# A planned order for the expert layer: routing in two parts, one-hots on VectorE, two sums for the gathered rows

## Chip, cores and metric

One Trainium2 chip, one core. The metric is the device time of one execution in microseconds (us), shown as the median of several runs; the lower the better.

## What is computed

Two transformer blocks on one sequence of 256 tokens of width 2048. The first block has two layers (sparse attention beside retention), the second a mixer of two attentions and then PEER, a layer that picks single-neuron experts. The change lies in PEER alone. Cut to what matters:

```python
def peer_sublayer(h, w_query, sub_keys, u, v):       # 256 tokens, 8 heads, 16384 experts
    q = (hb @ w_query).reshape(PEER_BLOCK, 8, 2, 128)
    s = jnp.einsum('thpc,hpnc->thpn', q, sub_keys)    # two halves of 128 keys each
    top_s, top_i = lax.top_k(s, 16)
    cand_s = top_s[:, :, 0, :, None] + top_s[:, :, 1, None, :]
    best_s, best_j = lax.top_k(cand_s.reshape(..., 256), 16)
    idx = take_along_axis(128 * first_half + second_half, best_j)
    g = softmax(best_s)
    a = gelu(einsum('thkd,td->thk', u[idx], hb))
    return einsum('thk,thkd->td', g * a, v[idx])
```

## The kernel before

The work up to the queries (both attention blocks, `first_layer`, `second_mixer`) is ordered by the framework's scheduler, and so is PEER. PEER goes through these steps, in tiles of 128 tokens by `t` in 0 and 1:

- **Queries and routing** (`peer_query`, `peer_route`). Four chunks of the query weight, each split into a high and a low part for exact products (`raw`, `hi`, `lo`, L204 and L205). For each of 16 pairs of head and token tile `peer_route` takes two top-16 of 128 keys (`top16`), adds them to 256 sums, takes their top-16, marks the places (`eq`, a product on GpSimd), reduces to key numbers (`keyno`) and row numbers (`idx`), and makes the softmax weights `gw`. `digit_rows` splits the key numbers into digits for the distance products below.
- **Scores.** The first `GU` = 1024 columns of the table `u` are fetched row by row for the picked experts: `peer_gather_u`, 256 indirect DMAs from GpSimd's queue of 128 rows each (L1307), whose product with `hn` is summed on VectorE (L1315, "dot") or multiplied on GpSimd (L1312) and summed on ScalarE (L1313), by a fixed turn. The last 1024 columns go dense through TensorE: `peer_scores` loads 128 pieces `uraw`, turns each (L259), splits it (`uhi` L1337 on ScalarE, `ulo` L1338 on VectorE) and multiplies (L1340 to L1342) into `S`. The text calls one piece an expert (it holds 128 of them).
- **Picks and weights.** `peer_pick` draws the scores of the picked experts out of `S` by one-hot products (`ohf`, L1359; selection L1363), `peer_coef` makes the coefficients `cf`, and `peer_weights` builds two one-hots per token from distance products on TensorE (L1389, L1395), multiplies them (L1400) and moves the result back over `S` (L1401). 32 groups of four tokens for each `t`.
- **Output.** The table `v` in the same two ways: `peer_gather_v` fetches `GV` = 704 columns by 256 indirect DMAs (L1415) and adds them, weighted, to one sum `vacc`, on VectorE (L1424) or by a scaling on ScalarE (L1421) and an add on GpSimd (L1422), by a fixed turn; `peer_out` loads 128 pieces `vraw` of the other 1344 columns, splits them and `S` (`vhi`, `vlo` L1441, `wh`, `wl` L1445) and multiplies (L1449).

Indirect rows land in rings of buffers that are taken in turn (`gathered_rows`): three, later six. SP's queue issues all plain loads in order. `ahead` mixes gathers into the dense steps at fixed rates, and the scheduler may lift them ahead:

```python
def ahead(self, gather, n=1):
    with self.tc.high_priority(offset=AHEAD):
        for _ in range(n):
            next(gather, None)
```

## Time and profile before

| | before |
|---|---|
| median of 3 runs (lowest, highest) | 3316.0 us (3314.67, 3328.48) |
| the profiled execution's own time | 3326.01 us |
| its span, first to last instruction | 3324.3 us |
| mean granted TensorE clock | 0.945 |
| busy: TensorE, VectorE, ScalarE, GpSimd | 90%, 71%, 48%, 36% |
| moved by DMA | 749.43 MB, 225 GB/s on average |

The profile is of one execution. A busy share is an average over stages with different limits, so it is read by stretch. Where instructions of one engine overlap, its busy time counts the union. In single rows the first number is the start in us from the span's start, the second the duration, then engine, source line, operation and tiles.

### The profile page before, as it was taken

To read this page: it belongs to the slowest core of one execution; us is meant where nothing else is said; L and a number is where in the kernel's file an instruction comes from. 1 tells how busy PE (TensorE), PEld (TensorE's weight loads), DVE (VectorE), ACT (ScalarE), POOL (GpSimd) and SP (SyncE) were. 2 spreads that over 40 slices of the span, in tenths; PEclk is the share of its full clock that TensorE was granted. 3 is DMA by queue.
4 is the path that set the end of the run, shared out by engine and by line. 5 is a ranking of instruction groups with operands and counts; after the bars stand their busy time and mean duration, and the time that the engine had idled before them with its cause. 6 is when DMAs were issued, how large, how long until landed. Compare 5 with 4: busy or idle time off the path is not lost.

```text
span 3324.3 us, 46436 instructions
## 1 busy us (share of the span) xinstructions
PE 2992.6 (90%) x16644; PEld 2519.5 (76%) x16644; DVE 2357.7 (71%) x4263; ACT 1583.7 (48%) x2533; POOL 1205.5 (36%) x861
## 2 busy tenths in 40 slices
PE   3698999799999999999999578889888999999998
PEld 1476667577788779998779567888787778788887
DVE  7879886967766664565558998777554565888886
ACT  5555545545444544454544233433333466555553
POOL 3324432412000000000002645776554346877772
PEclk9699998899999999999999799999998996999999
DMA  8777876767655555544466668999884234999997
GB/s 299 236 248 248 282 252 199 250 188 222 174 165 159 167 163 150 150 139 134 145 226 194 209 222 269 335 341 334 268 275 163 73 114 140 324 330 325 322 335 250
DMA packets 294612, 749.43 MB, mean 225 GB/s; under 512 B 33518, under 2 KB 40612, under 8 KB 293996
## 3 DMA queue, kind: packets, MB, share of 16 engines
q1 hardware_dynamic: 236432, 517.74, 49.0%
q0 software_dynamic: 57344, 226.53, 19.7%
q8 instruction: 131, 2.15, 0.3%
q10 hardware_dynamic: 604, 2.19, 0.2%
q14 instruction: 101, 0.83, 0.1%
HBM read 739.55 MB, written 6.82 MB: 225 GB/s over the span
## 4 chain that ended last, share of the span: by engine, by line
PE 56%; DMA 13%; DVE 13%; POOL 5%; issue 5%; ACT 3%; POOLq 0%; another core or an unknown queue 0%; DVEq 0%; ACTq 0%; SPq 0%
PE b_mm L1449 10%; PE b_mm L231 7%; PE b_mm L230 7%; PE b_mm L232 7%; DMA mraw<-in_w_mod 6%; DMA gathered<-in_peer_u,idx 5%; PE b_at L1359 4%; PE b_at L1449 3%; DVE gathered L1315 3%; PE b_tr L1400 3%; DVE lo L205 2%; PE b_mm L252 2%; PE b_mm L251 2%; PE b_mm L250 2%; POOL gathered L1307 2%
## 5 line engine op out<-in xcount | busy, mean ns | idle before, releaser
L205 DVE TENSOR_TENSOR lo<-raw,hi 128x1024 fp32r<-128x1024 f32 (+2 forms) x488 | 615.0, 1262 | 360.1 <-ACT hi L204 358.1
L204 ACT CAST hi<-raw 128x1024 fp32r<-128x1024 f32 (+2 forms) x488 | 498.8, 1025 | 486.0 <-PE b_mm L232 275.4
L231 PE MATMUL b_mm<-lo,hh 128*128 128x512 f32 (+1 forms) x1536 | 620.3, 404 | 29.6 <-DVE lo L205 29.0
L232 PE MATMUL b_mm<-hi,hl 128*128 128x512 f32 (+1 forms) x1536 | 605.0, 399 | 0.0
L230 PE MATMUL b_mm<-hi,hh 128*128 128x512 f32 (+1 forms) x1536 | 581.6, 402 | 9.0 <-ACT hi L204 6.7
L1342 PE MATMUL b_mm<-hd,ulo 128*128 128x256 f32 x1024 | 315.3, 308 | 80.2 <-DVE ulo L1338 78.9
L1415 POOL DMA_INDIRECT gathered<-in_peer_v,idx x256 | 333.2, 1302 | 144.6 <-DVE vacc L1424 92.3
L231 PEld LDWEIGHTS b_mm<-lo,hh 128*128 128x128 f32 x1536 | 295.5, 192 | 109.8 <-DVE lo L205 50.0
L1307 POOL DMA_INDIRECT gathered<-in_peer_u,idx x256 | 286.5, 1119 | 252.1 <-DVE gathered L1315 140.2
L230 PEld LDWEIGHTS b_mm<-hi,hh 128*128 128x128 f32 x1536 | 293.6, 192 | 84.2 <-ACT hi L204 11.2
L232 PEld LDWEIGHTS b_mm<-hi,hl 128*128 128x128 f32 x1536 | 294.0, 192 | 62.3 <-issue 0.8
L1340 PE MATMUL b_mm<-hd,uhi 128*128 128x256 f32 x1024 | 317.8, 310 | 21.7 <-ACT uhi L1337 20.9
L398 POOL TENSOR_TENSOR macc<-macc,mraw 128x512 f32<-128x512 f32 x112 | 182.2, 1627 | 422.9 <-ACT mraw L396 382.9
L1315 DVE SCALAR_TENSOR_TENSOR gathered<-gathered,hn 128x1024 f32<-128x1024 f32 x196 | 264.1, 1354 | 83.3 <-DMA gathered<-in_peer_u,idx 83.2
L1341 PE MATMUL b_mm<-hd,uhi 128*128 128x256 f32 x1024 | 299.9, 293 | 0.0
L1342 PEld LDWEIGHTS b_mm<-hd,ulo 128*128 128x128 f32 x1024 | 207.0, 202 | 101.0 <-DVE ulo L1338 98.9
L1337 ACT CAST uhi<-b_tr 128x512 fp32r<-128x512 f32 x256 | 148.6, 587 | 260.5 <-PE b_tr L259 224.0
L1338 DVE TENSOR_TENSOR ulo<-b_tr,uhi 128x512 fp32r<-128x512 f32 x256 | 174.3, 687 | 105.1 <-ACT uhi L1337 93.9
L1441 DVE TENSOR_TENSOR vlo<-vraw,vhi 128x1344 fp32r<-128x1344 f32 x128 | 206.8, 1616 | 34.5 <-ACT vhi L1440 31.8
L1340 PEld LDWEIGHTS b_mm<-hd,uhi 128*128 128x128 f32 x1024 | 206.7, 202 | 29.4 <-ACT uhi L1337 27.2
L1341 PEld LDWEIGHTS b_mm<-hd,uhi 128*128 128x128 f32 x1024 | 207.0, 202 | 0.0
L1424 DVE SCALAR_TENSOR_TENSOR vacc<-gathered,cf,vacc 128x704 f32<-128x704 f32 x186 | 177.2, 953 | 19.7 <-POOL vacc L1422 10.4
(608 smaller groups left out, 6248.4 us busy)
## 6 DMA issues: line engine op xcount, KB each, us to landing
raw<-in_w_in SPq DMA_DIRECT2D x336, 512.0 KB
mraw<-in_w_mod SPq DMA_DIRECT2D x192, 512.0 KB
vraw<-in_peer_v SPq DMA_DIRECT2D x128, 672.0 KB
uraw<-in_peer_u SPq DMA_DIRECT2D x128, 512.0 KB
raw<-in_w_out SPq DMA_DIRECT2D x96, 512.0 KB
raw<-in_peer_w_query SPq DMA_DIRECT2D x32, 512.0 KB
raw<-in_w_in SPq DMA_DIRECT2D x16, 256.0 KB
gathered<-in_peer_u,idx POOLq DMA_INDIRECT x256
```

The lines of the kernel that those rows point to most:

```text
L204: nc.scalar.copy(hi[:, :, :n], raw[:, :, :n])
L205: nc.vector.tensor_tensor(lo[:, :, :n], raw[:, :, :n], hi.bitcast(F32)[:, :, :n], ALU.subtract)
L230: nc.tensor.matmul(o, ah[:, kk, s], hi[:, k, :n], start=kk == 0, stop=False)
L231: nc.tensor.matmul(o, ah[:, kk, s], lo[:, k, :n], start=False, stop=False)
L232: nc.tensor.matmul(o, al[:, kk, s], hi[:, k, :n], start=False, stop=kk == KT - 1)
L1307: nc.gpsimd.indirect_dma_start(out=g, out_offset=None, in_=rows, in_offset=bass.IndirectOffsetOnAxis(ap=self.idx[h, t][:, k:k + 1], axis=0))
L1315: nc.vector.scalar_tensor_tensor(g, g, 1.0, self.hn[:, t, :], op0=ALU.mult, op1=ALU.mult, accum_out=o)
L1340: nc.tensor.matmul(o, hi[:, k, :], hh[:, k0 + k, :], start=k0 + k == 0, stop=False)
L1341: nc.tensor.matmul(o, hi[:, k, :], hl[:, k0 + k, :], start=False, stop=False)
L1342: nc.tensor.matmul(o, lo[:, k, :], hh[:, k0 + k, :], start=False, stop=k0 + k == UD - 1)
L1415: nc.gpsimd.indirect_dma_start(out=g, out_offset=None, in_=rows, in_offset=bass.IndirectOffsetOnAxis(ap=self.idx[h, t][:, k:k + 1], axis=0))
L1449: nc.tensor.matmul(acc[t, q][:, :w], a[:, t * P:(t + 1) * P], b[:, c - GV:c - GV + w], start=e == 0 and n == 0, stop=e == P - 1 and n == 2)
```

## The change

From the queries on, the order of every engine's instructions is fixed in the kernel. A new class `Plan` takes each step as an operation with an engine (or a choice of two), a cost, a key of priority, what it follows and which ring of buffers it takes and frees. `Plan.run` keeps one clock per engine and one for DMA, always emits the step that can start first (the smallest key within 0.05 us), and the framework keeps that order (`manual_schedule`).

With it:

- Routing is in two parts (`plan_route`): the two top-16 of a pair go ahead with early keys, the sums and the rest follow with later ones, nine pairs of results deep. Marks are one `eq` of two halves in bf16. The softmax weights are divided once per `t`.
- Products with gathered `u` rows and sums of gathered `v` rows have no fixed turn: the plan chooses between VectorE on the one side and GpSimd with ScalarE on the other. GpSimd's sums of `v` go to a second accumulator, merged at the end. Gather buffers are taken in any order.
- Weights: the two one-hots of a token are made on VectorE by comparing with a row of numbers; their distance products on TensorE are gone, and with them half of the digit rows.
- `GV` goes from 704 to 768, so the dense part of `v` from 1344 to 1280 columns. Five pieces of `u` are loaded ahead into buffers of their own (`PRE`), and the transposes use a second pair of banks from the 17th piece on.

In numbers, from the built order: gather products on VectorE 196 before, 159 now, on GpSimd 60 and 97; `v` adds on VectorE 186 and 100, on ScalarE and GpSimd 70 and 156 (of these 154 adds on GpSimd); query subtractions on GpSimd none and 11 of 32; distance products 512 of 128x128 and none. In the output stage the built order has 93 adds on VectorE and 107 scalings on ScalarE.

```diff
+class Plan:
+    LAT = 0.15
...
+    def run(self):
+        while self.left:
+            best = None
+            for e, ops in self.ready.items():
...
+                first = min(c[0] for c in can) + 0.05
+                c = min((c for c in can if c[0] <= first), key=lambda c: c[1])
+                if best is None or c[0] < best[0]:
+                    best = c
...
+            end = self.clock[e] = t + cost
+            fn(o)
+            self.signal(o.issued, end, e)
+            if kb:
+                self.transfers = max(self.transfers, t) + kb / 340.0
+                end = max(self.transfers + 2.0, end + 3.5)
...
-GV = 704
+GV = 768
...
+        u = plan.op("DVE", 1.75, lambda o: best_half(o, 0), a0, after=[y], takes=[tv])
+        v = plan.op("DVE", 1.75, lambda o: best_half(o, 1), a0, after=[u], frees=[(sc, y)])
+        w = plan.op("DVE", 0.85, sums, b0, after=[v], takes=[cand, two], frees=[(tv, u)])
+        z = plan.op("DVE", 2.4, best_sums, b0, after=[w], frees=[(cand, w)])
+        b = plan.op("DVE", 1.3, places, b0, after=[z], takes=[eq])
+        m = plan.op("POOL", 1.8, marked, b0 - 20, after=[b])
...
-                    if k % (3 if self.gathered < 56 else UOFF if self.gathered < 240 else 2) == 1:
-                        nc.gpsimd.tensor_tensor(g, g, self.hn[:, t, :], ALU.mult)
-                        nc.scalar.activation(g, g, AF.Identity, accum_out=o)
-                    else:
-                        nc.vector.scalar_tensor_tensor(g, g, 1.0, self.hn[:, t, :], op0=ALU.mult,
-                                                       op1=ALU.mult, accum_out=o)
+                plan.choice([("DVE", 1.42, dot, (), 0), ("POOL", 2.5, product, (poolq,), 0)], key, after=[o])
...
-            r1, r, c = self.distance(t, n)
-            p1 = self.bank("mm", 4)
-            for i in range(4):
-                nc.tensor.matmul(p1[:, i * P:(i + 1) * P], r1[:, i * P:(i + 1) * P], c, start=True, stop=True)
+            def second(o, n=n, s=s):
+                s["b"] = self.vp.tile([P, 4, P], F32, name="ohb", tag="ohb", bufs=3)
+                nc.vector.tensor_tensor(s["b"], self.iota[:, None, :].to_broadcast([P, 4, P]),
+                                        self.byexp[t][:, 1, n:n + 4, None].to_broadcast([P, 4, P]), ALU.is_equal)
+            def first(o, n=n, s=s):
+                s["a"] = a = self.vp.tile([P, 4, P], F32, name="oha", tag="oha", bufs=4)
+                for i in range(4):
+                    nc.vector.tensor_scalar(a[:, i, :], self.iota, self.byexp[t][:, 0, n + i:n + i + 1],
+                                            self.byexp[t][:, 2, n + i:n + i + 1], op0=ALU.is_equal, op1=ALU.mult)
...
-                    if k % VOFF == 1 and not (t == 1 and h >= 6):
-                        nc.scalar.activation(g, g, AF.Identity, scale=c)
-                        nc.gpsimd.tensor_tensor(a, a, g, ALU.add)
-                    else:
-                        nc.vector.scalar_tensor_tensor(a, g, c, a, op0=ALU.mult, op1=ALU.add)
+                            plan.op("POOL", 2.05, lambda o: nc.gpsimd.tensor_tensor(a, a, s["g"], ALU.add), key - 12,
+                                    after=[o], frees=[(gv, s["op"]), (poolq, o)], signals=[self.added])
...
+                    plan.choice([("DVE", 1.06, add, (), 0), ("ACT", 0.98, scale, (poolq,), 0)], key,
+                                after=[o, self.cf_done[t][1]])
```

Three places of the built order. First SP's queue of loads, from the last weights of the mixer to the score table (`raw` are weights of the mixer and of the queries, `uraw` and `upre` pieces of the score table). Before:

```order
L199 DMA raw<-in_w_out 128x2x512 x10
L1327 DMA uraw<-in_peer_u 128x1024 x3
L199 DMA raw<-in_w_out 128x2x512 x22
L199 DMA raw<-in_peer_w_query 128x2x512 x5
...
L1175 DMA x_kept<-x 128x4096
...
L199 DMA raw<-in_peer_w_query 128x2x512 x27
L1327 DMA uraw<-in_peer_u 128x1024 x24
```

Now:

```order
L355 DMA raw<-in_w_out 128x2x512 x32
L1457 DMA raw<-in_peer_w_query 128x2x512 x3
...
L1332 DMA x_kept<-x 128x4096
...
L1711 DMA upre_14666<-in_peer_u 128x1024
L1711 DMA uraw<-in_peer_u 128x1024 x3
L1457 DMA raw<-in_peer_w_query 128x2x512 x29
L1711 DMA uraw<-in_peer_u 128x1024 x33
```

Five pieces `upre` and three `uraw` now stand behind the first three query weights.

Second, VectorE where routing and scores share it (`ulo` is the score subtraction, `gathered` the product with a gathered row, `cand`, `best`, `bj`, `eq`, `keyno`, `idx` belong to routing). Before:

```order
L1315 SCALAR_TENSOR_TENSOR gathered,act_14636<-gathered,hn 128x1024
L1500 CAST bf__16425<-bj 128x32
L1221 TENSOR_SCALAR dig<-dig 128x128
L1338 TENSOR_TENSOR ulo<-b_tr,uhi 128x512
L1504 TENSOR_TENSOR eq<-bf__16425,iota_14622 128x256 x2
L1222 TENSOR_SCALAR dig<-dig 128x128
L1338 TENSOR_TENSOR ulo<-b_tr,uhi 128x512
```

Now:

```order
L1575 TENSOR_REDUCE keyno_14631<-eq 128x2x16
L1578 SCALAR_TENSOR_TENSOR idx<-keyno_14631 128x16
L1579 TENSOR_SCALAR idx<-idx 128x16
L1731 TENSOR_TENSOR ulo<-b_tr,uhi 128x512
L2018 MAX best<-cand 128x8
L2019 MAX_INDEX bj<-best,cand 128x8
L2021 MATCH_REPLACE cand<-best,cand 128x256
L2018 MAX best<-cand 128x8
L2019 MAX_INDEX bj<-best,cand 128x8
L1731 TENSOR_TENSOR ulo<-b_tr,uhi 128x512
```

Before, 49 `ulo` and 50 products stand ahead of the last `idx`; now 72 `ulo` and 11 products. GpSimd has 43 gathers and 30 products ahead of its last mark, and 215 gathers of `u` ahead of the first of `v`.

Third, GpSimd in the output stage. Before:

```order
L1415 DMA gathered<-in_peer_v,idx 128x704 x3
L1422 TENSOR_TENSOR vacc<-vacc,gathered 128x704
L1415 DMA gathered<-in_peer_v,idx 128x704 x4
L1422 TENSOR_TENSOR vacc<-vacc,gathered 128x704
L1415 DMA gathered<-in_peer_v,idx 128x704 x3
```

Now:

```order
L1921 TENSOR_TENSOR vacc_22893<-vacc_22893,gathered 128x768
L1902 DMA gathered<-in_peer_v,idx 128x768 x2
L1921 TENSOR_TENSOR vacc_22893<-vacc_22893,gathered 128x768
L1902 DMA gathered<-in_peer_v,idx 128x768
L1921 TENSOR_TENSOR vacc_22893<-vacc_22893,gathered 128x768
```

An add stood behind every third or fourth gather; now behind every one or two, and it has a sum of its own. Of the 64 weight groups on TensorE 18 stand between picks and 46 behind the last pick.

## Rows read from the trace of the kernel before

**Rows 1.** Busy time of each engine by stretch (us from the span's start):

```profile
core 0: us, PE busy (x) PEld busy (x) DVE busy (x) ACT busy (x) POOL busy (x), PEclk, DMA share, GB/s
1740.00:2037.00 297.00, 223.97 (x1646) 211.86 (x1646) 265.79 (x818) 105.03 (x203) 143.56 (x116) 0.90 0.65 212
2037.00:2541.00 504.00, 435.89 (x3323) 415.18 (x3324) 331.35 (x525) 188.82 (x340) 310.84 (x230) 0.94 0.86 303
2541.00:2626.00 85.00, 82.95 (x351) 60.73 (x350) 43.13 (x292) 30.07 (x54) 15.68 (x11) 0.94 0.15 46
2626.00:2743.00 117.00, 115.77 (x735) 91.28 (x736) 74.03 (x276) 70.24 (x101) 63.02 (x54) 0.96 0.43 124
2743.00:2828.00 85.00, 80.74 (x518) 69.17 (x516) 42.50 (x65) 56.01 (x78) 52.54 (x42) 0.64 0.49 142
2828.00:3314.00 486.00, 481.59 (x2304) 405.09 (x2304) 405.04 (x395) 257.08 (x302) 345.50 (x226) 0.99 0.91 318
```

**Rows 2.** Timeline of TensorE, scores: transpositions of one half piece each:

```profile
2305.57 0.60 PE L259 MATMUL b_tr<-ident,uraw 128*128 128x128 f32 x4
...
2309.32 0.60 PE L259 MATMUL b_tr<-ident,uraw 128*128 128x128 f32 x4
```

**Rows 3.** The chain that ended last, 2330 to 2400 us: shares, one piece:

```profile
by line: DMA gathered<-in_peer_u,idx 55.6%; issue 11.7%; DVE gathered L1315 11.4%; POOL gathered L1312 7.0%; POOL gathered L1307 5.4%; DVE ulo L1338 2.7%; PE b_mm L1342 2.7%; PE b_mm L1340 2.0%; PE b_mm L1341 1.9%; PE b_tr L259 1.9%; ACT uh
...
2338.75 8.72 DMA gathered<-in_peer_u,idx
```

**Rows 4.** Groups by line, 2037 to 2541 us (busy, mean ns | idle before):

```profile
L1307 POOL DMA_INDIRECT gathered<-in_peer_u,idx x186 | 209.7, 1128 | 170.9 <-DVE gathered L1315 117.9 <-issue 32.0 <-ACT gathered L1313 9.1
L1315 DVE SCALAR_TENSOR_TENSOR gathered<-gathered,hn 128x1024 f32<-128x1024 f32 x146 | 198.7, 1370 | 65.5 <-DMA gathered<-in_peer_u,idx 65.5
L1338 DVE TENSOR_TENSOR ulo<-b_tr,uhi 128x512 fp32r<-128x512 f32 x208 | 141.5, 688 | 105.1 <-ACT uhi L1337 93.9 <-issue 9.0 <-ACT S L1344 1.6
```

**Rows 5.** The page's 40 slices; tile raw: ns min/median/max, first and last start:

```profile
GB/s 299 236 248 248 282 252 199 250 188 222 174 165 159 167 163 150 150 139 134 145 226 194 209 222 269 335 341 334 268 275 163 73 114 140 324 330 325 322 335 250
...
L205 DVE TENSOR_TENSOR lo<-raw,hi x488: 135/1225/3006, 35.6 to 1855.6; 128x1024 fp32r<-128x1024 f32 x156, 128x672 fp32r<-128x672 f32 x5, 128x16 fp32r<-128x16 f32 x2
```

**Rows 6.** Picks (group, 2541 to 2626 us), weight products (timeline), a tensor_scalar (group):

```profile
L1359 PE MATMUL b_at<-S,ohf 128*128 128x128 f32 x288 | 71.9, 406 | 0.5 <-ACT ohf L1356 0.5
...
2692.95 1.16 PE L1400 MATMUL b_tr<-ohb,oha 128*128 128x128 f32 x8
...
2748.32 2.08 PE L1400 MATMUL b_tr<-ohb,oha 128*128 128x128 f32 x8 [0.47 <-DVE ohb L1391]
...
L1224 DVE TENSOR_SCALAR digf<-digf 128x128 f32<-128x128 f32 x4 | 0.9, 216 | 0.0
```

**Rows 7.** Timelines of VectorE and GpSimd, each at two places:

```profile
2089.66 3.24 DVE L1315 SCALAR_TENSOR_TENSOR gathered<-gathered,hn 128x1024 f32<-128x1024 f32 x1
2093.44 1.21 DVE L1315 SCALAR_TENSOR_TENSOR gathered<-gathered,hn 128x1024 f32<-128x1024 f32 x1
...
2898.76 1.56 DVE L1441 TENSOR_TENSOR vlo<-vraw,vhi 128x1344 fp32r<-128x1344 f32 x1 [0.45 <-ACT vhi L1440]
2901.19 0.98 DVE L1445 TENSOR_TENSOR wl<-S,wh 128x256 fp32r<-128x256 f32 x1 [0.88 <-PE b_at L1449]
...
2089.40 2.41 POOL L1312 TENSOR_TENSOR gathered<-gathered,hn 128x1024 f32<-128x1024 f32 x1
...
2899.59 2.30 POOL L1422 TENSOR_TENSOR vacc<-vacc,gathered 128x704 f32<-128x704 f32 x1 [0.40 <-ACT gathered L1421]
```

**Rows 8.** Groups by line, 2828 to 3314 us, output stage:

```profile
L1441 DVE TENSOR_TENSOR vlo<-vraw,vhi 128x1344 fp32r<-128x1344 f32 x128 | 206.8, 1616 | 34.5 <-ACT vhi L1440 31.8 <-issue 2.7
...
L1424 DVE SCALAR_TENSOR_TENSOR vacc<-gathered,cf,vacc 128x704 f32<-128x704 f32 x136 | 129.8, 955 | 6.8 <-DMA gathered<-in_peer_v,idx 6.6
L1422 POOL TENSOR_TENSOR vacc<-vacc,gathered 128x704 f32<-128x704 f32 x47 | 94.2, 2003 | 32.1 <-ACT gathered L1421 30.5 <-DVE vacc L1424 0.7 <-issue 0.5
...
L1445 DVE TENSOR_TENSOR wl<-S,wh 128x256 fp32r<-128x256 f32 x128 | 87.0, 680 | 40.8 <-PE b_at L1449 31.8 <-ACT wh L1444 8.7
```

More of the change, by code (lines that the diff above doesn't have):

```diff
@@ L1 @@
-import itertools
 import math
@@ L44 @@
 GU = D - UD * P
-GV = 704
+GV = 768
 GMAX = max(GU, GV)
+FOUR = [P, 2, TOPK, TOPK]
+PRE = 5
+URAW = 3
 UBUFS = 3
-AHEAD = 100
-VOFF = 3
-UOFF = 6
-FIRST = 16
+VRAW = 4
 _INS = (
@@ new lines, in open_scores, with open_more, leave_ud @@
+    def open_scores(self, o):
+        self.st.close()
+        self.st = ExitStack()
+        self.S = self.pool(self.st, "Sp").tile([P, P, T], F32, name="S")
+    def open_more(self, o):
+        self.qs.close()
+        self.rg = self.pool(self.st, "rg")
+        self.gu.add([(self.rg, "g%d" % i) for i in range(3)], self.plan.now)
+    def leave_ud(self, o):
+        more = [s for s in self.gu.slots if s[1][0] is self.rg]
+        self.gu.slots = [s for s in self.gu.slots if s[1][0] is self.ud]
+        self.gu.retire(self.plan, self.left_ud)
+        self.gu.slots += more
@@ L1285, in ahead @@
-    def ahead(self, gather, n=1):
-        with self.tc.high_priority(offset=AHEAD):
-            for _ in range(n):
-                next(gather, None)
-    def gathered_rows(self):
-        turn = itertools.chain.from_iterable([r] * r[1] for r in self.rings)
-        pool, n = next(itertools.islice(turn, self.turn % sum(n for _, n in self.rings), None))
-        self.turn += 1
-        return pool.tile([P, GMAX], F32, name="gathered", tag="g", bufs=n)
-    def peer_gather_u(self):
-        nc = self.nc
-        self.gathered = self.turn = 0
-        rows = self.I["peer_u_2"][0].rearrange("n (c w) -> (n c) w", w=UNIT)
+        return self.rows[p, 512 * h:512 * h + 512], self.digits[p, 4 * t + q, :]
@@ L1303, in peer_gather_u, with plan_gather_v @@
+    def plan_gather_v(self, units, chosen):
+        nc, plan, gv = self.nc, self.plan, self.gv
+        rows = self.I["peer_v_2"][0].rearrange("n (c w) -> (n c) w", w=UNIT)
+        n, last = 0, [chosen]
+        poolq = self.ring("poolv", 2)
         for t in range(2):
@@ new lines, in plan_gather_v, with plan_out, start @@
+                    s["op"] = o = plan.op("POOL", 1.08, gather, key - 25, after=last, takes=[gv], kb=GV / 2)
+                    last = [o.issued]
+                    plan.choice([("DVE", 1.06, add, (), 0), ("ACT", 0.98, scale, (poolq,), 0)], key,
+                                after=[o, self.cf_done[t][1]])
+                    n += 1
+    def plan_out(self, opened):
+        nc, plan, ring = self.nc, self.plan, self.ring
+        cols = [(c, min(512, D - c)) for c in range(GV, D, 512)]
+        acc = {}
+        wide = D - GV
+        def start(o):
@@ L1453, in peer_out @@
-            for _ in gather:
-                pass
-            for t in range(2):
-                for q, (c, w) in enumerate(cols):
-                    y = vp.tile([P, D - GV], F32, name="y", tag="vraw", bufs=4)[:, :w]
-                    nc.sync.dma_start(y, self.x_kept[:, t, c:c + w])
-                    nc.vector.tensor_tensor(y, y, acc[t, q][:, :w], ALU.add)
-                    nc.sync.dma_start(self.out[0, t * P:(t + 1) * P, c:c + w], y)
-                nc.sync.dma_start(self.out[0, t * P:(t + 1) * P, :GV], self.vacc[:, t, :])
+        first = plan.op("ctl", 0, start, 0, after=[opened], takes=[ring("mm", 4)] * 4 + [ring("at", 2)] * 2)
```

934 lines of the change are left out of this document (647 added, 287 removed).

## The prediction, made before the changed kernel was run

> **What bounds the kernel now.** I read the stretches first, then in each of them the groups and single rows of the work that paces it. The change starts at the queries (1740 us), and the built order of all five engines is unchanged ahead of them, so 1740 us stay. Behind them come three stages [rows 1]: queries, routing and scores to 2541 (801 us), picks and weights to 2828 (287 us), the output stage to 3314 (486 us), and 10 us of stores.
>
> In the first, VectorE is busy for 266 of the 297 us to 2037 and TensorE for only 224: with routing and score work in one queue, only some 25 of 128 experts are scored by then (in the built order 49 score subtractions stand ahead of the last routing instruction). Between 2037 and 2541 neither is full: TensorE 436 of 504, DMA at 303 GB/s. Where TensorE is fed, one expert passes in 3.75 us, from one transposition to the second next [rows 2], but 104 experts took 504 us, 4.85 each. The chain of waits names the cause: more than half of a stretch there is landing time of gathered rows [rows 3]. The 186 gathers of this stretch [rows 4] are 2.71 us apart; six buffers make that a loop of 6 x 2.71 = 16 us from one use of a buffer to its next.
>
> In the output stage TensorE is busy for 482 of 486 us: it sets the pace, with DMA close behind at 318 GB/s.
>
> **The change, part by part.** *Queries and routing to 2000 us.* In the new order the first halves of the routing stand ahead of the scores and the second halves between them; 72 score subtractions, 36 experts, now stand ahead of the last routing instruction, and 11 gather products of VectorE instead of 50. The queries themselves keep their 118 us to 1858 (the last weight split starts at 1855.6 [rows 5]). On SP's queue eight pieces of the score table, 4.2 MB, now stand behind the first three query weights and ahead of the other 29 (now three of them stand further ahead), 14 us at 303 GB/s; I take nothing for them, since TensorE works on the three pieces and VectorE, not TensorE, ends this stretch, and 14 us as the upper end. What VectorE has left of the routing at 1858: of its 266 us take 32 query subtractions at 1.23 = 39, 50 products at 1.37 = 68 and 49 score subtractions at 0.68 = 33 [rows 4]; 126 remain for routing and normalisation, and some six tenths of the routing instructions now stand behind the first score, about 75 us. With 72 x 0.68 = 49 and 11 x 1.37 = 15 that is 139 us, against TensorE's 36 x 3.75 = 135. So 36 experts are done near 2000, where now there are 25 at 2037.
>
> *Scores to 2415 us.* 92 experts remain. GpSimd has issued 43 of the 256 gathers by then and 215 before the first gather of the next table: 172 in this stretch. By TensorE alone 92 x 3.75 = 345 us. By DMA: 92 + 172 pieces of 0.524 MB = 138 MB, 457 us at the 303 GB/s of now and 406 at the 341 that the best slice of the profile's page shows [rows 5]. By the loop of buffers, at 2.71 us, 466. A buffer is now taken as soon as the plan has it free, not in turn, and VectorE does 131 products instead of 196 before the picks, so I put the loop nearer to the DMA's end: 415 us, ends 345 and 466. First stage 675 us (now 801): **minus 126**.
>
> *Picks and weights.* The picks keep their instructions: the first stretch had 36 of them (288 half matmuls of eight to a pick [rows 6]) in 85 us, 2.36 each, so 64 cost 151. For the weights the 512 distance matmuls go, and the products stay: eight half matmuls take 1.16 us at full clock and 2.08 at half clock [rows 6]. The granted clock was 0.96 where picks and weights alternated and 0.64 where weights stood alone [rows 1]. In the new order 18 groups of four tokens stand between picks and 46 behind the last: 18 x 1.16 + 46 x 2.08 = 117. VectorE makes the one-hots: four tensor_scalar of 128x128, nearest row 0.216 us [rows 6], and one 128x512, nearest row 0.68 [rows 4], 1.55 us a group. It is hidden under 2.08; were the clock full, it would pace the last 46 groups, 71 us in place of 96. Sum 268, I take 265; ends 240 and the 287 of now: **minus 22**.
>
> *Output stage.* The table's direct part shrinks from 1344 to 1280 columns and the gathered part grows from 704 to 768. TensorE's 482 us become 482 x 1280/1344 = 459. But in the built order only 56 of the 256 gathered rows are added before the stage, so 200 are left in it: 128 x 0.655 + 200 x 0.393 = 163 MB, against the 155 MB that 318 GB/s made in 486 us. That is 511 us at 318 and 477 at 341.
>
> The third limit is what this change moves most. GpSimd's adds of gathered rows go from 70 to 154, 107 of them in this stage (now 47 [rows 8]), each preceded by a ScalarE scaling, and they go into a sum of their own, so that they no longer wait for VectorE's. The trace shows that a GpSimd operation and a VectorE operation with two SBUF inputs don't run together [rows 7]: a product of 1.22 us took 3.24, its start within a GpSimd product that ended at 2091.81; an add that began inside a subtraction ended 1.57 us after it (2901.89 against 2900.32); and the short subtraction behind it ended 0.28 us after the add. By these net times, with widths scaled: 128 x 1.56 x 1280/1344 = 190, 128 x 0.28 = 36, VectorE's 93 adds x 0.955 [rows 8] x 768/704 = 97, GpSimd's 107 x 1.57 x 768/704 = 183: **506 us** in which one excludes the other, more than TensorE's 459. The same sum for now is 200 + 36 + 136 x 0.955 + 47 x 1.57 = 440 of 486. So I take 510 us; ends 459 (it all hides) and 570 (the means of [rows 8], which hold some of the waiting, give 128 x (1.616 x 0.95 + 0.68) + 97 + 107 x 2.003 x 768/704 = 615; I cap it short of them since they count a wait on both engines). **Plus 24.** The Trainium skill, SBUF — State Buffer, "Who interferes with whom", calls this shared port pair an exclusive lock, held for the whole instruction by whoever starts first; the trace agrees in [rows 7]. A plan that knows no lock would count the two engines side by side, and the stage at TensorE's 459.
>
> **Sum.** 1740 + 675 + 265 + 510 + 10 = 3200 us of span, 3202 with the 1.7 us around it, against 3326 of the profiled execution: 124 us less, 3.7%. The median of the three runs is 3316, 10 below the profiled one, so I forecast **3190 us**.
>
> **Rivals.** *All of it hides* (15%). The scores run at 4.0 us an expert, the weights at full clock, the output stage at TensorE's 459: 1740 + 628 + 240 + 465 + 10 = 3083, or about 3075. For it speaks that single slices reached 341 GB/s; against it that three stages must all meet their floor.
>
> *The lock eats the gain* (20%). GpSimd also makes 97 products instead of 60 in the score stage, and VectorE's queue stands still behind each that it meets; the scores keep their loop of 2.71 us (726 us) and the output stage takes 570: 1740 + 726 + 275 + 570 + 10 = 3321, no change, or with one of the two only 3250. For it: [rows 7], and it is what the lock of that page of the Trainium skill would do here. Against it: in the score stage the sum is only 172 products in all on two engines at 1.2 to 2.4 us, some 260 of 415 us.
>
> *Slower: the loop of gather buffers* (10%). VectorE's order is now fixed by planned clocks; a gather that lands later than planned stops every score subtraction behind it, and with them TensorE. A landing in the chain is 8.7 us long [rows 3]. If a gather costs 3.2 us instead of the 415/172 = 2.4 that I take, 138 us are lost and the gain is gone; at 3.5 us the first stage is 862 us and the time 3377. For it: that chain. Against it: the order of now is as fixed, and the new one has fewer products of VectorE to stop at.
>
> That the change doesn't do what it says is settled for the order (it is built so); whether the clocks behind it hold is what the rivals are about.
>
> **How the numbers follow.** My forecast has 55% (3130 to 3260). Differences under 0.5%, 17 us, can hardly be told from no change here. Faster by more: the forecast, the first rival and half of the second, 80%. Within 0.5%: most of the rest of the second, 8%. Slower: the last rival and the tail of the second, 12%. The range leaves out the slowest tenth and a tenth at the fast end: 3090 to 3300.
>
> **What would show it.** The last score product near 2415 us, the first output product near 2680, the last near 3190; in the output stage some 107 GpSimd adds, stretched beyond 1.9 us, and TensorE with idle time that VectorE's subtractions end; DMA near 320 GB/s there; the granted clock near half in the last 46 weight groups. I am wrong if the scores take under 4 or over 5 us an expert, or if the output stage takes 465 us with the GpSimd adds stretched all the same.

## The result, and the profile after

The changed kernel takes 3367.0 us (median of 4 runs, 3363.3 to 3370.8) against 3315.3 before (4 runs, 3311.3 to 3328.5): a ratio of 1.0149, 95% interval 1.0118 to 1.0180. It is 1.5% slower; 3190 was forecast. The profiled execution is that of 3370.8 us, span 3369.1.

With the stages bounded by the end of the last copy of scores and that of the last copy of weights (the first stage counted from 1740 us):

| us | before | forecast | after |
|---|---|---|---|
| queries, routing, scores | 801 | 675 | 717 |
| picks and weights | 286 | 265 | 345 |
| output stage, with tail | 497 | 520 | 567 |

The first stage gained 84 us, two thirds of the forecast. The other two gave back 59 and 70. Stretches of the changed kernel, columns as in [rows 1]:

```profile
1740.00:1870.00 130.00, 107.92 (x838) 104.76 (x838) 101.22 (x279) 54.83 (x91) 55.59 (x33) 0.89 0.57 187
1870.00:2457.00 587.00, 523.29 (x4136) 502.76 (x4135) 502.63 (x822) 263.03 (x506) 439.68 (x306) 0.97 0.83 291
2457.00:2590.00 133.00, 98.02 (x380) 73.82 (x381) 87.96 (x388) 47.42 (x83) 93.36 (x66) 0.72 0.58 190
2590.00:2683.00 93.00, 72.30 (x343) 59.82 (x343) 92.27 (x278) 47.34 (x62) 69.57 (x50) 0.85 0.41 118
2683.00:2813.00 130.00, 70.06 (x373) 63.52 (x371) 122.34 (x246) 64.56 (x74) 78.44 (x54) 0.70 0.37 114
2813.00:3358.00 545.00, 479.17 (x2304) 389.79 (x2304) 501.75 (x349) 297.54 (x360) 481.10 (x301) 0.97 0.86 294
```

Before, TensorE was busy for 95% or more of every one of the last four stretches of [rows 1]. Now VectorE (third busy column) comes first in two of them: 92 of 93 us where picks and weights alternate, 122 of 130 where weights stand alone, while TensorE is busy for 72 and 70. In the output stage VectorE and GpSimd are busy for 502 and 481 of 545 us, and TensorE, with 479 us of work, waits. What fills VectorE in the last weights, groups by line, 2683 to 2813 us:

```profile
L1864 DVE TENSOR_SCALAR oha<-iota,byexp 128x128 f32<-128x128 f32 x175 | 86.7, 558 | 0.0
L1870 PE MATMUL b_mm<-oha,ohb 128*128 128x128 f32 x368 | 69.3, 359 | 47.1 <-DVE ohb L1858 35.0 <-DVE oha L1864 8.2 <-ACT S L1874 3.4
...
L1921 POOL TENSOR_TENSOR vacc<-vacc,gathered 128x768 f32<-128x768 f32 x24 | 45.8, 1909 | 21.6 <-ACT gathered L1916 21.2
...
L1858 DVE TENSOR_TENSOR ohb<-iota,byexp 128x512 f32<-128x512 f32 x44 | 32.2, 739 | 0.0
```

The one-hots of some 44 groups of four tokens take 86.7 + 32.2 us of VectorE's time here, 2.7 us a group. (Busy times are used, since neighbouring one-hots overlap and their means add up to more.) Of the 47 us for which TensorE stood idle in front of its products, 43 end with a one-hot. The timeline shows what stretches them, first VectorE, then GpSimd, each with start, duration and operation:

```profile
2740.34 1.10 DVE L1864 TENSOR_SCALAR oha<-iota,byexp 128x128 f32<-128x128 f32 x4
2741.97 8.96 DVE L1864 TENSOR_SCALAR oha<-iota,byexp 128x128 f32<-128x128 f32 x8
...
2742.90 1.81 POOL L1921 TENSOR_TENSOR vacc<-vacc,gathered 128x768 f32<-128x768 f32 x1
2745.97 1.81 POOL L1921 TENSOR_TENSOR vacc<-vacc,gathered 128x768 f32<-128x768 f32 x1
2749.03 1.81 POOL L1921 TENSOR_TENSOR vacc<-vacc,gathered 128x768 f32<-128x768 f32 x1
```

Four one-hots took 1.10 us alone; eight took 8.96 beside three additions, which were not slowed themselves. The output stage, groups by line, 2813 to 3358 us, against [rows 8]:

```profile
L1957 DVE TENSOR_TENSOR vlo<-vraw,vhi 128x1280 fp32r<-128x1280 f32 x128 | 268.2, 2096 | 3.9 <-ACT vhi L1953 3.7
...
L1921 POOL TENSOR_TENSOR vacc<-vacc,gathered 128x768 f32<-128x768 f32 x107 | 213.8, 1999 | 2.2
L1970 PE MATMUL b_mm<-vlo,wh 128*128 128x512 f32 x512 | 166.2, 417 | 65.7 <-DVE vlo L1957 65.6
...
L1909 DVE SCALAR_TENSOR_TENSOR vacc<-gathered,cf,vacc 128x768 f32<-128x768 f32 x91 | 141.5, 1555 | 26.7 <-DMA gathered<-in_peer_v,idx 26.5
L1965 DVE TENSOR_TENSOR wl<-S,wh 128x256 fp32r<-128x256 f32 x126 | 110.4, 876 | 10.9 <-PE b_at L1970 7.0 <-ACT gathered L1916 1.2 <-ACT wh L1961 0.2
```

The table subtraction has fewer columns than before and takes 2.10 us instead of 1.62; VectorE's addition takes 1.56 instead of 0.96. All of TensorE's 65.7 us of idle time in front of these products ends with that subtraction.

### The profile page after: what moved, and what is told of

It reads as the page before. It is cut to its first block, busy times and chain, and to the rows that moved or that the text cites. A ratio compares the mean times of both kernels' runs of the same rounds, so it can differ in the third digit from the quotient of the medians.

```text
span 3369.1 us, 45653 instructions
## 1 busy us (share of the span) xinstructions
PE 2915.7 (87%) x16134; PEld 2456.3 (73%) x16134; DVE 2602.2 (77%) x4256; ACT 1646.7 (49%) x2629; POOL 1492.3 (44%) x994
## 3 DMA queue, kind: packets, MB, share of 16 engines
q8 instruction: 127, 2.08, 0.3%
## 4 chain that ended last, share of the span: by engine, by line
PE 38%; DVE 20%; DMA 12%; POOL 12%; issue 10%; ACT 3%; POOLq 0%; DVEq 0%; SPq 0%; ACTq 0%
PE b_mm L387 7%; PE b_mm L386 7%; PE b_mm L388 7%; DMA mraw<-in_w_mod 6%; PE b_mm L1970 4%; DMA gathered<-in_peer_u,idx 3%; POOL gathered L1686 3%; POOL vacc L1921 3%; POOL gathered L1674 3%; DVE vlo L1957 2%; POOL gathered L1902 2%; PE b_mm L408 2%; PE b_mm L406 2%; PE b_mm L407 2%; DVE lo L361 2%
## 5 line engine op out<-in xcount | busy, mean ns | idle before, releaser
L361 DVE TENSOR_TENSOR lo<-raw,hi 128x1024 fp32r<-128x1024 f32 (+2 forms) x456 | 571.6, 1255 | 351.9 <-ACT hi L360 349.9
L360 ACT CAST hi<-raw 128x1024 fp32r<-128x1024 f32 (+2 forms) x456 | 464.6, 1021 | 453.6 <-PE b_mm L388 275.9
L1680 DVE SCALAR_TENSOR_TENSOR gathered<-gathered,hn 128x1024 f32<-128x1024 f32 x159 | 284.3, 1802 | 65.7 <-DMA gathered<-in_peer_u,idx 65.5
L1741 PE MATMUL b_mm<-hd,ulo 128*128 128x256 f32 x1024 | 301.8, 295 | 27.3 <-DVE ulo L1731 26.5
L1739 PE MATMUL b_mm<-hd,uhi 128*128 128x256 f32 x1024 | 308.6, 301 | 10.4 <-ACT uhi L1727 10.0
L1921 POOL TENSOR_TENSOR vacc<-vacc,gathered 128x768 f32<-128x768 f32 x154 | 302.0, 1961 | 33.4 <-ACT gathered L1916 30.4
L1740 PE MATMUL b_mm<-hd,uhi 128*128 128x256 f32 x1024 | 294.2, 287 | 0.0
L1957 DVE TENSOR_TENSOR vlo<-vraw,vhi 128x1280 fp32r<-128x1280 f32 x128 | 268.2, 2096 | 3.9 <-ACT vhi L1953 3.7
L1686 POOL TENSOR_TENSOR gathered<-gathered,hn 128x1024 f32<-128x1024 f32 x97 | 235.7, 2430 | 24.5 <-DMA gathered<-in_peer_u,idx 19.7
L1970 PE MATMUL b_mm<-vlo,wh 128*128 128x512 f32 x512 | 166.2, 417 | 65.7 <-DVE vlo L1957 65.6
L1739 PEld LDWEIGHTS b_mm<-hd,uhi 128*128 128x128 f32 x1024 | 201.0, 196 | 14.4 <-ACT uhi L1727 14.3
L1740 PEld LDWEIGHTS b_mm<-hd,uhi 128*128 128x128 f32 x1024 | 201.2, 196 | 0.0
```

Of the source, the lines that this page charges most:

```text
L360: nc.scalar.copy(hi[:, :, :n], raw[:, :, :n])
L361: nc.vector.tensor_tensor(lo[:, :, :n], raw[:, :, :n], hi.bitcast(F32)[:, :, :n], ALU.subtract)
L1686: nc.gpsimd.tensor_tensor(s["g"], s["g"], self.hn[:, t, :], ALU.mult)
L1739: nc.tensor.matmul(o, h["hi"][:, k, :], hh[:, kk, :], start=kk == 0, stop=False)
L1740: nc.tensor.matmul(o, h["hi"][:, k, :], hl[:, kk, :], start=False, stop=False)
L1741: nc.tensor.matmul(o, h["lo"][:, k, :], hh[:, kk, :], start=False, stop=kk == UD - 1)
```

## The experiments

Theory L: VectorE's operations with operands in SBUF and GpSimd's exclude each other, and the 154 additions on GpSimd cost more than they take off VectorE. Rivals: W, VectorE has too much one-hot work of its own; D, the 200 gathered rows of the output stage set it; F, the fixed order stops at rows that land late. Unless an interval stands beside it in the text, a time is one execution; the kernel before, run beside them, gave 3295.0 to 3327.3 in all. Executions of one changed kernel lay up to 10 us apart, so single times closer than that are not told apart. Stages as in the table above:

| us | time | first | picks, weights | output, tail |
|---|---|---|---|---|
| e1_no_pool_sum | 3198.6 | 707 | 274 | 476 |
| e2_second_on_pe | 3358.8 | 716 | 361 | 539 |
| e3_vector_adds | 3242.7 | 713 | 278 | 509 |
| e4_landing | 3395.3 | 719 | 346 | 588 |
| e5_dots_vector | 3217.2 | 689 | 275 | 511 |
| e6_adds_third | 3272.5 | 713 | 279 | 539 |
| e7_second_pe_vadds | 3245.3 | 719 | 289 | 495 |
| e8_gv704 | 3256.2 | 711 | 277 | 526 |
| e10_digits_second | 3216.0 | 698 | 290 | 491 |
| e11_no_pool_arith | 3225.1 | 700 | 275 | 512 |
| e12_port_plan | 3367.0 | 732 | 300 | 600 |
| e13_port_landing | 3344.7 | 695 | 329 | 579 |
| e14_vadds_landing | 3245.0 | 716 | 277 | 509 |
| e15_port_vadds | 3276.9 | 735 | 287 | 513 |

### e1_no_pool_sum: the additions on GpSimd left out, all else in its order

The rows that ScalarE scales are fetched and scaled as before and then missing from the output, so e1 is a bound and no kernel to use.

```diff
-plan.op("POOL", 2.05, lambda o: nc.gpsimd.tensor_tensor(a, a, s["g"], ALU.add), key - 12,
+plan.op("POOL", 2.05, lambda o: None, key - 12,
```

> Leaves out GpSimd's 154 additions of scaled rows of the second table (so the rows that ScalarE scales are missing from the output); the planned order of everything else is kept. Theory L (VectorE and GpSimd exclude each other): the table subtraction falls from 2.10 us to 1.5, the short subtraction from 0.88 to 0.42, VectorE's additions from 1.56 to 1.05; the output stage falls from 545 us to 470-485, the last 46 weight groups from 130 us to 95-105; time about 3265. Theory D (the output stage waits for 200 gathered rows, 163 MB): the stage stays over 530, time over 3340. Theory W (VectorE has too much one-hot work of its own): the weight groups stay at 125 us or more, with VectorE full.

Tiles `vlo`, `wl` and `oha` in the trace of e1 (least, median and longest, ns; first and last start), then its stretch of weights and its output stage, then one group of one-hots and the start of the next on VectorE's timeline:

```profile
L1957 DVE TENSOR_TENSOR vlo<-vraw,vhi x128: 1476/1484/1495, 2732.8 to 3179.9; 128x1280 fp32r<-128x1280 f32 x128
L1965 DVE TENSOR_TENSOR wl<-S,wh x128: 416/425/426, 2721.2 to 3178.7; 128x256 fp32r<-128x256 f32 x128
L1864 DVE TENSOR_SCALAR oha<-iota,byexp x256: 327/334/550, 2575.0 to 2717.3; 128x128 f32<-128x128 f32 x128
```

```profile
2646.00:2721.00 75.00, 54.33 (x362) 48.64 (x360) 74.93 (x226) 61.72 (x72) 26.29 (x23) 0.91 0.47 135
2721.00:3186.00 465.00, 453.71 (x2304) 384.55 (x2304) 327.15 (x355) 298.08 (x362) 289.17 (x200) 0.98 0.97 353
```

```profile
2658.58 0.68 DVE L1858 TENSOR_TENSOR ohb<-iota,byexp 128x512 f32<-128x512 f32 x1
2659.18 1.10 DVE L1864 TENSOR_SCALAR oha<-iota,byexp 128x128 f32<-128x128 f32 x4
2660.20 0.68 DVE L1858 TENSOR_TENSOR ohb<-iota,byexp 128x512 f32<-128x512 f32 x1
```

The same order is 172 us shorter in span. No subtraction of 128 takes longer than 1.495 us, where their mean was 2.096. VectorE's busy time in the output stage fell from 502 to 327 us. The weights fell by 55 us, more than expected. VectorE is still full there (74.9 of 75 us), so its own one-hot work sets the 75 us, at 1.62 us a group; W does not explain the 130. D is out: the same 256 rows were gathered, and the stage took 465 us at 353 GB/s. ScalarE's 154 scalings were kept, so they are not the cost either.

### e2_second_on_pe and e4_landing: two misses with the additions kept

e2, in `plan_weights` (`apart` makes four distance products of 128 columns into `s["pd"]`; `second` is a ScalarE Relu of them):

```diff
-            a = plan.op("DVE", 0.64, second, key - 6, after=[coef[2]], takes=[rb])
+            tr = ring("tr", 2)
+            q = plan.op("PE", 0.45, apart, key - 8, after=[coef[2], self.far, self.rowed], takes=[tr])
+            a = plan.op("ACT", 0.62, second, key - 6, after=[q], takes=[rb], frees=[(tr, q)])
```

e4, in `Plan.run`:

```diff
-                end = max(self.transfers + 2.0, end + 3.5)
+                end = max(self.transfers + 5.5, end + 7.0)
```

> The one-hot of the second key goes back to TensorE's distance products and a ScalarE Relu; the coefficient's one-hot stays on VectorE; the planner lays all out anew. It takes 0.74 to 0.94 us from VectorE in each of 64 groups. Theory W: the last 46 groups go to TensorE's 2.1 us each, 97 us instead of 130, picks and weights together from 356 to 310; time about 3325. Theory L: the four remaining operations keep 0.55 to 0.70 us each, so 46 x 4 x 0.6 = 110 us and picks and weights 330; the output stage stays at 540 to 550; time about 3345. If neither (the second ring of banks or ScalarE binds): 3369 or more.

> One number: the planner takes a transfer to land 7.0 us after its issue instead of 3.5 (and 5.5 after the transfers ahead of it instead of 2.0), so that VectorE's products of gathered rows are laid out later. Theory F (the fixed order stops at rows that land later than planned): VectorE's idle time in front of gathered rows, 43 us in the scores and 24 in the picks, falls to under 25 together, the picks' stretch from 133 us to 110, time about 3340. Theory L: the idle time falls, but the time stays within 10 us of 3369.

e2 gained 8 us, within what single executions differ by, where both theories said 22 or more. The planner used VectorE's free time for 46 additions of rows in the last weights, and the coefficient's one-hots still took 0.533 us each there; picks and weights became 361 us. In e4 VectorE's idle time in front of the first table's rows fell from 24 to 0.6 us in the picks, as F expects, and the time rose by 28 us: products that had stood in the picks now met the additions (the last one begins at 2694 instead of 2594 us). Planning with a later landing takes that wait away and does not mend the picks and weights.

### e3_vector_adds and e6_adds_third: none, or a third, of the rows to GpSimd

```diff
-plan.choice([("DVE", 1.06, add, (), 0), ("ACT", 0.98, scale, (poolq,), 0)], key,
+plan.choice([("DVE", 1.06, add, (), 0)], key,
```

The merge of the second sum goes with it. In e6 the choice stays for every third row:

```diff
+plan.choice([("DVE", 1.06, add, (), 0), ("ACT", 0.98, scale, (poolq,), 0)][:1 + (k % 3 == 1)], key,
```

> All 256 rows of the second table are added by VectorE, none by ScalarE and GpSimd, one sum; planned anew. Theory L: VectorE's work in the output stage runs at its clean prices, 128 x (1.50 + 0.42) + 200 x 1.04 = 454 us, the stage 480 to 500, time about 3300 to 3315. Rival (VectorE was relieved by GpSimd's additions on balance): the stage is set by VectorE and its waits for rows, 560 or more, time over 3385.

> The changed kernel with only every third row free to go to ScalarE and GpSimd: 59 additions on GpSimd instead of 154, 195 on VectorE instead of 100. Theory L with a price for each addition: (3369 - 3243) / 154 = 0.82 us each, 3243 + 59 x 0.82 = 3291. Rival (up to some number the additions hide in VectorE's waits): 3250 or less. Rival (any such addition upsets the fixed order): 3340 or more.

e3 computes everything, is faster than both kernels, and is below the range of L, whose sum had counted the output stage alone: picks and weights fell as well, from 345 to 278 us. Groups by line in its output stage, 2731 to 3229 us:

```profile
L1902 POOL DMA_INDIRECT gathered<-in_peer_v,idx x242 | 339.8, 1404 | 95.4 <-DVE vacc L1909 65.2 <-issue 25.0 <-DMA gathered<-in_peer_v,idx 1.9
L1909 DVE SCALAR_TENSOR_TENSOR vacc<-gathered,cf,vacc 128x768 f32<-128x768 f32 x246 | 249.1, 1013 | 7.5 <-DMA gathered<-in_peer_v,idx 5.3
L1957 DVE TENSOR_TENSOR vlo<-vraw,vhi 128x1280 fp32r<-128x1280 f32 x128 | 189.9, 1484 | 12.6 <-ACT vhi L1953 12.6
```

VectorE does 246 additions there instead of 91, and is busy for 460 us of 498, where it was busy for 502 of 545. Taking 154 additions from GpSimd saved 3369 - 3240 = 129 us of span, 0.84 each. e6's 59 cost 30 us more than e3, 0.51 each instead of the 0.82 expected, between the forecasts of theory and rivals; most of that is rows left over behind the last product (the last addition begins at 3263 us, the last product at 3240). The price is not linear.

### e5_dots_vector and e11_no_pool_arith: the first stage

e5 is e3 with the first pair of lines, e11 with both changes and, in `open_pick`, the load of `spread` moved ahead of that of `vacc`:

```diff
-plan.choice([("DVE", 1.42, dot, (), 0), ("POOL", 2.5, product, (poolq,), 0)], key, after=[o])
+plan.choice([("DVE", 1.42, dot, (), 0)], key, after=[o])
-c = plan.choice([("DVE", 1.28, lambda o, f=lo: f(o, nc.vector), (), 0),
-                 ("POOL", 2.5, lambda o, f=lo: f(o, nc.gpsimd), (), 0)], key - 80, after=[b],
+c = plan.choice([("DVE", 1.28, lambda o, f=lo: f(o, nc.vector), (), 0)], key - 80, after=[b],
```

> As e3_vector_adds, and all 256 products of the first table's gathered rows on VectorE too, so that GpSimd has none of the 97. Theory L (the exclusion also slows routing and scores): the products fall from a mean of 1.80 us to 1.23, the routing's small operations to their medians, the last score copy comes before 2440 us instead of 2452, time about 3225. Rival V (VectorE has no room for 97 more products, 119 us): the last score copy after 2475 or the picks longer, time over 3265. Rival D (TensorE and the transfers set the scores at 333 GB/s whoever multiplies): 3243 within 10.

> As e5_dots_vector, with all 32 query splits on VectorE too (17 there, 15 on GpSimd), so that GpSimd keeps only the gathers and the routing's small products; and the small table of digits is loaded ahead of the 0.8 MB that start the sum, at the head of the picks. Theory L: the splits' longest of 3.40 us falls to 1.3 and the queries end some 5 us sooner, the picks start 3 us sooner: 3217 - 8 = 3209. Rival V (VectorE paces the queries, 15 x 1.23 = 18 us more of it): the last query split at 1865 or later, 3220 to 3230. Against the kernel before at 3315: a ratio near 0.970.

The group of the products in the changed kernel, 2037 to 2457 us; then the same operation by tile in e5, and e5's stretch of scores:

```profile
L1680 DVE SCALAR_TENSOR_TENSOR gathered<-gathered,hn 128x1024 f32<-128x1024 f32 x121 | 226.2, 1884 | 42.9 <-DMA gathered<-in_peer_u,idx 42.8
```

```profile
L1680 DVE SCALAR_TENSOR_TENSOR gathered<-gathered,hn x256: 1207/1225/1873, 1915.5 to 2529.9; 128x1024 f32<-128x1024 f32 x128
```

```profile
2037.00:2432.00 395.00, 367.30 (x2988) 361.77 (x2987) 349.72 (x610) 129.96 (x238) 241.84 (x189) 0.96 0.96 366
```

97 more products on VectorE make the first stage 24 us shorter than in e3, as L has it. VectorE's products took 1.88 us on average between 2037 and 2457 us of the changed kernel; in e5 their median is 1.225 us and the longest 1.873. TensorE and the transfers did not set 333 GB/s; they went to 366. In e11 the splits' longest fell to 1.226 us and the last began at 1851 us, as expected, yet the time is 3225 us (3220 to 3229, 6 runs, ratio to before 0.9744, interval 0.9718 to 0.9770): nothing gained over e5's single 3217. The first stage took 700 us against e5's 689 although the queries ended sooner. Rival V's time came without its sign (a last split at 1865 or later), so why nothing was gained stays open.

### e7_second_pe_vadds, e8_gv704, e10_digits_second: the other parts, without GpSimd's additions

e7 is e3 with e2's edit, e10 is e5 with e2's edit and `spread` loaded first, and e8 is e3 with

```diff
-GV = 768
+GV = 704
```

> As e3_vector_adds, with the one-hot of the second key made by TensorE's distance products and ScalarE. VectorE, which is full in the last 46 weight groups (79 of 79 us), is rid of 0.685 us a group. If VectorE's work paces them: 46 groups in 60 to 65 us, the stretch of mixed picks and weights 62 instead of 72, time about 3217. If the granted clock falls (0.70 where VectorE was stretched): 46 x 2.1 = 97 us, time about 3260.

> As e3_vector_adds, with the gathered part 704 columns wide as before the change instead of 768. If TensorE sets the output stage: 470 x 1344/1280 = 494, about 24 us more, time about 3266. If the transfers set it (363 GB/s, 180.5 MB against 176.6): 11 us less, time about 3232. If both are near: 3243 within 8.

> As e5_dots_vector, with the small table of digits loaded first at the head of the picks, and the one-hot of the second key on TensorE and ScalarE as in e7_second_pe_vadds. There it moved VectorE's time from the weights to the gathered rows and gained nothing (3245 against 3243). If that holds whatever the first stage does: 3217 - 3 = 3214 within 8. If the shorter first stage lets TensorE's 457 us set the output stage as in e7 without longer weights: 3195.

Where the one-hot of the second key is made matters little without GpSimd's additions: e7 is within 3 us of e3, and e10 within 2 us of e5. Neither forecast for e7 came. In e7 the time that VectorE got free went to rows again: weights 11 us longer, output 14 us shorter, with TensorE busy for 457 of 465 us. The wider gathered part is worth some 13 us (one execution each), between the forecasts of e8: its TensorE has 487 us of work in its stage against 470, so the likely reading is that TensorE set most of it. e10 is the fastest of the kernels that compute everything: 3216 us (3211 to 3220, 4 runs), ratio to before 0.9714, interval 0.9680 to 0.9747. So the new order, without arithmetic for GpSimd on gathered rows, is 2.6% (e11) to 2.9% (e10) faster than before, and up to 4.5% faster than the change as it is (3216 / 3367).

### e12 to e15: telling the planner of the exclusion

```diff
+    def port(self, a):
+        return a[0] == "POOL" and a[1] > 1.5 or a[0] == "DVE" and not hasattr(a[2], "psum")
...
 def start(self, o, a):
     t = max(self.clock[a[0]], o.ready)
+    if self.port(a):
+        t = max(t, self.shared)
```

`shared` is set to the end of each such operation in `run`; `low.psum = True` and `select.psum = True` mark the two that read PSUM, and `first` is priced at 1.35 instead of 0.9. e13 is e12 with e4's edit, e14 is e3 with e4's edit, e15 is e12 with e3's edit.

> The changed kernel with the exclusion written into the planner: arithmetic on GpSimd and every VectorE operation but those that read PSUM (the score subtraction and the selection of the picks) share one more clock, and the coefficient's one-hot is priced at 1.35 us instead of 0.9. The planner then gives GpSimd 21 additions instead of 154 and 70 products instead of 97, and no query split. Theory L: this mends most of the loss without a choice being forbidden: between e3_vector_adds and e5_dots_vector, 3215 to 3245. Rival (the fixed order fails for landings and other clocks that the planner still has wrong): 3290 or more.

> As e12_port_plan, with a transfer taken to land 7.0 us after its issue instead of 3.5. In e12_port_plan GpSimd had only 21 additions and VectorE's operations ran at clean prices, yet the output stage took 589 us: VectorE stood 87 us in front of rows that had not landed, and the next gathers stood 256 us behind VectorE's additions for a buffer. Theory F (with the exclusion planned, the landing is the clock that is wrong): that idle time falls under 30 us, the output stage to 500-520, time 3280 to 3300. Rival (a few GpSimd additions in the fixed order are enough to upset it): the stage stays over 560, time over 3345.

> As e3_vector_adds (3243 us, no additions on GpSimd), with the landing of 7.0 us. Theory F: its order has VectorE behind the rows already (7 us idle in front of rows of the second table), so the output stage stays within 10 us of 498; the first stage, with 95 us of idle time in front of rows of the first table, gains up to 20: 3223 to 3243. Rival (a longer landing holds buffers longer and starves the gathers, as e4_landing's 26 us more may say): over 3260.

> As e12_port_plan (exclusion in the planner, landing 3.5 us), with the 21 additions that it left on GpSimd taken to VectorE as well; 71 products stay on GpSimd. If the few additions upset the fixed order: the output stage falls from 589 us to about 500 and VectorE's 87 us in front of rows of the second table to under 20, time 3260 to 3290 (the first stage is 19 us longer than in e3_vector_adds). If it is the planned landing, whoever adds: the stage stays over 560, time over 3340.

e12 is a miss of the theory: 3367.0 us (4 runs, ratio 1.0165, interval 1.0137 to 1.0193), no better than the change, with its VectorE operations at clean prices. Gathers and additions in its output stage, 2773 to 3362 us, then those of e15, 2773 to 3262 us:

```profile
L1914 POOL DMA_INDIRECT gathered<-in_peer_v,idx x232 | 304.9, 1314 | 288.7 <-DVE vacc L1921 255.8 <-DMA gathered<-in_peer_v,idx 15.1 <-issue 11.3
L1921 DVE SCALAR_TENSOR_TENSOR vacc<-gathered,cf,vacc 128x768 f32<-128x768 f32 x232 | 236.9, 1021 | 92.6 <-DMA gathered<-in_peer_v,idx 87.3 <-issue 4.3 <-DVE wl L1977 0.2
```

```profile
L1914 POOL DMA_INDIRECT gathered<-in_peer_v,idx x236 | 333.1, 1411 | 97.7 <-DVE vacc L1921 58.3 <-issue 31.7 <-DMA gathered<-in_peer_v,idx 4.3
L1921 DVE SCALAR_TENSOR_TENSOR vacc<-gathered,cf,vacc 128x768 f32<-128x768 f32 x241 | 244.6, 1015 | 5.4 <-DMA gathered<-in_peer_v,idx 3.0
```

VectorE waited 87 us for rows, and the next gathers waited 256 us for VectorE to free a buffer: a loop of buffers, in the output stage. Forbidding its 21 additions on GpSimd (e15, planned anew) took 90 us off and the wait with it. Why 21 cost more here than 59 in e6 can be seen in the trace of e12: all scalings of rows on ScalarE (count, durations, first and last start), then GpSimd's last four additions on its timeline, with gathers between them left out:

```profile
L1928 ACT ACTIVATE gathered<-gathered,cf x21: 918/928/935, 2583.8 to 2790.1; 128x768 f32<-128x768 f32 x21
```

```profile
2777.52 1.82 POOL L1933 TENSOR_TENSOR vacc<-vacc,gathered 128x768 f32<-128x768 f32 x1
...
2785.08 2.24 POOL L1933 TENSOR_TENSOR vacc<-vacc,gathered 128x768 f32<-128x768 f32 x1
...
3295.31 4.35 POOL L1933 TENSOR_TENSOR vacc<-vacc,gathered 128x768 f32<-128x768 f32 x2
```

All 21 rows were scaled by 2791 us, but two of them were added only from 3295 us on. A buffer is freed by the addition, so two of the six stood still for some 500 us and the other rows went round in four. In e6 no scaled row waits longer than 8 us for its addition, in the change as it is none longer than 16. The second loss is thus one of the plan and not of the additions' own time: it put two short steps off for a whole stage while they held buffers. The trace shows the two rows; that they make up the whole 90 us was not tested on its own. The later landing time (e13) has two such rows as well, put off for 470 us. It closed the gaps between TensorE's products but left rows for some 85 us behind the last one; without additions (e14) it changes nothing.

## Why the prediction was wrong, point by point

- *Queries and routing to 2000 us* was some 48 us optimistic: the last `idx` begins at 2048, and 33 experts were scored at 2037 where 36 were forecast near 2000. The queries ended some 12 us later than before, inside the upper end of 14 but by another way: 11 of their splits went to GpSimd, and VectorE's 21 took 1.66 us on average, not 1.23. GpSimd's products fall on the routing's small operations too: a 128x32 cast took up to 4.07 us, median 0.23. Without GpSimd's products and additions (e5) the first stage still takes 689 us, so 14 of its 42 us over the forecast lie elsewhere and were not traced.
- *Scores, 4.5 us an expert*, held: 190 half pieces, 95 experts, in the 420 us from 2037, 4.42 each, at 331 GB/s. The stage ended late (2457 instead of 2415) because it began late.
- *Picks and weights, 265 us*, is the step that failed most: 345 to the last copy, 356 to the first output product. Two terms of it failed. The first is "hidden under 2.08". The exclusion, which the prediction read in [rows 7] and used in the output stage, was not applied to the one-hots, and the 47 of GpSimd's 154 additions that fall in these stages were not counted. Beside them a group took 2.7 us and the last weights 130 us, where 96 were forecast. The price itself, 1.55 us a group, was near: clean groups start 1.62 us apart in e1, and its last weights take 75 us.
- The second term is the price of a pick, 2.36 us. It came from a stretch with four gathers of the first table left in it; now 43 were left for the picks, and the prediction put nothing down for them. 333 half matmuls took 133 us, 3.2 us a pick, with TensorE busy for 98 of the 133 us at a granted clock of 0.72. The first table's rows in the picks, before (2541 to 2626 us) and now (2457 to 2590 us):

```profile
L1307 POOL DMA_INDIRECT gathered<-in_peer_u,idx x4 | 3.9, 969 | 18.2 <-ACT gathered L1313 17.9 <-issue 0.3
```

```profile
L1674 POOL DMA_INDIRECT gathered<-in_peer_u,idx x43 | 49.4, 1150 | 28.3 <-DVE gathered L1680 17.9 <-DVE pjunk L1804 4.3 <-issue 4.1
L1680 DVE SCALAR_TENSOR_TENSOR gathered<-gathered,hn 128x1024 f32<-128x1024 f32 x29 | 40.0, 1395 | 23.9 <-DMA gathered<-in_peer_u,idx 23.9
```

Of the 133 us, 11 pass ahead of the first pick, where the small table `spread` is now loaded; the prediction did not look at that move. The chain shows it:

```profile
2457.27 7.92 DMA spread<-const_spread
2465.31 1.24 DVE digits L1426
```

This loss does not come from the additions on GpSimd: in e1 324 half matmuls of the picks took 128 us. That the gathers left over are its main cause is read from these rows and was not tested by a run of its own. That e1 comes to 274 us for picks and weights, near the 265, is in part luck: the weights were shorter than forecast and the picks longer.

- *Output stage, 510 us*: 545. The mechanism was right; the size was nearer the upper end of 570. At the prices of e1 and of the GpSimd additions in the first timeline above (1.81 us), the sum of 506 becomes 128 x 1.484 + 128 x 0.425 + 91 x 1.012 + 107 x 1.81 = 530: the short subtraction, taken at 0.28 us, costs 0.425. The sum also left out VectorE's 27 us in front of rows, and GpSimd's gathers (267 us busy beside 214 of additions). DMA, priced at 477 to 511 us, was no limit: e3 moved 363 GB/s over the stage.
- *Rivals.* "The lock eats the gain" came nearest in total. Its output stage of 570 was measured at 545. Its 726 us for the first stage (717) agree by chance: it had 260 + 466 us at 5.07 us an expert, and 297 + 420 at 4.42 were measured. It lacked its own mechanism in the picks and weights, 275 (356 to 2813): 3321 - 9 - 25 + 81 = 3368. "Slower: the loop of gather buffers" did not decide this kernel (e4); a loop of buffers did hold up e12, in another stage and with two buffers out of use.
- *Of the signs named*, stretched additions (mean 2.0 us) and TensorE's idle time ended by VectorE's subtractions came. The clock in the last weights was granted at 0.70, not near half. DMA near 320 GB/s (294) and the three times (2415, 2680 and 3190; measured 2457, 2813 and 3358) did not come.

## What to carry to other kernels

Ask in every stage, not only the one under study, what runs beside an operation on the engine that it excludes, and what work an earlier stage leaves behind for this one. A planner that balances VectorE against GpSimd as if they ran side by side gives GpSimd work at a loss: here a 1.01 us addition on VectorE became a 1.86 us one on GpSimd that VectorE waited for, 0.84 us of span for each of 154. Writing the exclusion into the planner is not enough by itself (e12): look for short steps that the plan puts off while they hold buffers. Leave out the suspected work once with the order kept (e1) before rebuilding anything: it bounds the gain in one run.
